# A hybrid decoder layer on one core: scores of two attention units in a row, a new order of the attention stage's groups, and another set of first transfers

## The chip, the cores and the metric

One core of a Trainium2 chip runs the whole layer as one program. The metric is the device time of one execution in microseconds (us), lowest is best; the time before is the median of three runs. The profile is of one further execution. The engines are named as in the profile: PE (TensorE matmul), PEld (its weight loads), DVE (VectorE), ACT (ScalarE), POOL (GpSimd) and SP (SyncE, which here only issues transfers).

## The reference

One layer on x of 512 positions by 1024 channels, float32, cut to what matters:

```python
x = x + 0.5 * swiglu(rms_norm(x, ffn1_norm), ...)            # d_ff 2816
h = rms_norm(x, mix_norm)
xr, gate, q, k, v = split(h @ w_in)                          # 512 columns each
y_rnn = rg_lru(conv(xr), gates) * gelu(gate)
qh, kh = rms_norm(heads(q)) / 8, rms_norm(heads(k))          # 8 heads of 64
z = qh @ kh.T ; causal = k_pos < q_pos                       # stick-breaking attention
tail = reverse_cumsum(where(causal, log_sigmoid(-z), 0)) - itself
w = where(causal, exp(log_sigmoid(z) + tail), 0) ; y_att = w @ v
x = x + concat(rms_norm(y_rnn), rms_norm(y_att)) @ w_out
x = x + 0.5 * swiglu(rms_norm(x, ffn2_norm), ...)
```

## The kernel before

Everything is held transposed: channels on the 128 partitions, the 512 positions along the free axis, x as eight tiles `x[k]` of 128x512. Every float32 product is three matmuls on a high and a low part of each operand (`mm3`: high-high, low-high, high-low). ACT makes the high parts, DVE the low parts.

**The start.** `first_products()` computes gate and up products of the first three 128-column blocks of the first FFN, six PSUM banks at once, while weights and x arrive. It issues, for `kk` = 0 to 3, `x[2*kk]`, six pieces of weights of 128x256 (`raw[i]`, alternately from the gate and the up matrix) and `x[2*kk+1]`, all over SP's queue. A tile `vec` (128x66) holds the norm gains, convolution weights and biases; it comes over ACT's queue. The first products need the high part of `x[0]`, which ACT computes with a gain out of `vec` (`xh_a`, L157), and the high parts of the weights (`first_h`: DVE makes that of piece 0, ACT that of piece 1). Ahead of them PE runs `WARM` matmuls of 128x128 float32 on constants (each is two matmul records in the profile). SP then goes on with the weights of the FFN.

**The attention stage.** The eight heads are taken in four pairs. A unit is the query blocks 3, or 2, or 1 and 0 of one pair of heads, so there are twelve units, in the order 3_0, 2_0, 1_0, 3_2, 2_2, 1_2, 3_4 and so on to 1_6 (the first query block, then the first head of the pair; the program's tile names end in the same way). `STEPS` is a string written by hand; its letters set the order on PE, and `step()` keeps each group behind the one before:

- Z, `weigh`: scores of one unit, for two heads at once, each on 64 of the 128 rows of the PE array; a bfloat16 matmul (`fut_b`) adds the mask. Two banks of the four of tag "z". ACT then writes `s` (sigmoid of -z) and `be` (sigmoid of z), DVE a scan (`rest`, L971) and a product into `be` (L979). There are three buffers for `be`, two for `s`.
- W, `turn_weights`: the unit's weights are transposed on PE (128x128 matmuls, 6 or 8 of them, into two banks of tag "w") and copied by ACT into `wt` (L999).
- P, `attend`: values times weights of one pair, after the pair's three W; 16 matmuls into the one bank of tag "y". ACT makes `yah` (L1019) and a square of it, DVE `yal` (L1022).
- F: the recurrent half of the output projection for one block of 128 columns, 12 matmuls into the one bank of tag "o" (the second F takes a "w" bank), copied out by ACT (`yr`, L1061) and added to `x[k]` by DVE (L1062).
- C, `begin`: the attention half for a block of columns, but for the last pair of heads, 9 matmuls, into a "z" bank. S and R are the sums for the last norm and their spreading.

The order of instructions on ACT and DVE is not written out: the framework's scheduler lays it down when the program is built, and each engine then works strictly through its own list.

Of the kernel before, what the change touches and what calls it, by code (L numbers as in the profile page):

```python
# [8 lines left out]
F32 = mybir.dt.float32  # L9
# [6 lines left out]
P = 128  # L16
T = 512
D = 1024
KD = D // P
# [16 lines left out]
LATE = 3  # L36

WIDE = {p: "gu" if p in (6, 9) else "g" for p in range(PLAIN // 2, NF // 2)}
WARM = 9

STEPS = "ZFZFZWZFWZWFZWZPWZFWZWZPWZFWZWPWFCWFPCCSCR"


C_G1, C_GM, C_G2 = 0, 8, 16
# [2 lines left out]
NVEC = 66  # L50
# [3 lines left out]
def hybrid_layer_kernel(  # L54
    ctx: ExitStack,
    tc: tile.TileContext,
    xT: bass.AP,
    vecs: bass.AP,
    wg1: bass.AP,
    wu1: bass.AP,  # L60
    wd1: bass.AP,
# [9 lines left out]
    nc = tc.nc  # L71

    const = ctx.enter_context(tc.tile_pool(name="const", bufs=1))
    wpool = ctx.enter_context(tc.tile_pool(name="wpool", bufs=3))
    xpool = ctx.enter_context(tc.tile_pool(name="xpool", bufs=1))
# [14 lines left out]
    def f32(ap):  # L90
        return ap.bitcast(F32)

    def bank(name, tag="b"):
        return banks["pool"].tile([P, T], F32, tag=tag, name=name, bufs=banks["tags"][tag])
# [1 line left out]

    mhalf = const.tile([P, 8], F32, tag="mhalf", name="mhalf")
    nc.vector.memset(mhalf, -0.5)
    vec = const.tile([P, NVEC], F32, tag="vec", name="vec")
    nc.scalar.dma_start(vec, vecs)  # L100
    warm = const.tile([P, 8], F32, tag="warm", name="warm")
    nc.scalar.activation(warm, mhalf, AF.Sigmoid)
    ones = const.tile([P, P], F32, tag="ones", name="ones")
# [16 lines left out]
        halves_b.append(t)  # L120
    ident_b, fut_b = halves_b

    x = [xpool.tile([P, T], F32, tag=f"x{k}", name=f"x{k}") for k in range(KD)]


    def weights(src, name, n=KD * P, rows=1):
# [400 lines left out]
    pt = bank("warm")  # L527
    for _ in range(WARM):
        nc.tensor.matmul(pt[:, :P], ones, ones, start=True, stop=True)
    n1 = Normed("a")  # L530

    def first_products():

        with tc.tile_pool(name="first", bufs=1, reuse_waits="tile") as fi:
            ws = [(w, f) for f in range(3) for w in (wg1, wu1)]
            raw, hi, lo, pts = [], [], [], []
            last = None
            for i in range(len(ws)):
                raw.append(fi.tile([P, KD * P], F32, tag=f"wr{i}", name=f"first_r{i}"))
                hi.append(fi.tile([P, KD * P], F32R, tag=f"wh{i}", name=f"first_h{i}"))  # L540
                lo.append(fi.tile([P, KD * P], F32R, tag=f"wl{i}", name=f"first_l{i}"))
                pts.append(bank(f"first_p{i}", "by"[i // 4]))
            for kk in range(KD // 2):
                s = slice(2 * kk * P, (2 * kk + 2) * P)
                nc.sync.dma_start(x[2 * kk], xT[:, 2 * kk, :])
                for i, (w, f) in enumerate(ws):
                    nc.sync.dma_start(raw[i][:, s], w[f // 2][:, f % 2 * KD * P :][:, s])
                nc.sync.dma_start(x[2 * kk + 1], xT[:, 2 * kk + 1, :])
            for kk in range(KD // 2):
                s = slice(2 * kk * P, (2 * kk + 2) * P)  # L550
                ks = (2 * kk, 2 * kk + 1)
                for k in ks:
                    n1.add(x[k], vec[:, C_G1 + k : C_G1 + k + 1], k)
                    if k == ks[0]:
                        for i in range(len(ws)):
                            if i == 0 or kk == 0 and i % 2 == 0:
                                nc.vector.tensor_copy(hi[i][:, s], raw[i][:, s])
                            else:
                                copied = nc.scalar.copy(hi[i][:, s], raw[i][:, s])
                                last = copied if kk == 1 else last  # L560
                        for i in range(len(ws)):
                            nc.vector.tensor_sub(lo[i][:, s], raw[i][:, s], f32(hi[i][:, s]))
                if kk == KD // 2 - 2:
                    with tc.issue_after(last.ins):
                        for k in range(KD):
                            n1.square(x[k], k, nc.vector)
                for k in ks:
                    s = slice(k * P, (k + 1) * P)
                    if k == KD - 1:
                        n1.rsqrt(D)  # L570
                    for wp, xp in ((hi, n1.h), (hi, n1.l), (lo, n1.h)):
                        if k == KD - 1 and wp is lo:
                            n1.spread()
                        for i in range(len(ws)):
                            nc.tensor.matmul(  # L575
                                pts[i],
                                wp[i][:, s],
                                xp[k],
                                start=k == 0 and wp is hi and xp is n1.h,
                                stop=k == KD - 1 and wp is lo,  # L580
                            )
        return [(pts[i], pts[i + 1]) for i in range(0, len(ws), 2)]
# [3 lines left out]
    def into(norm, c, squares=True):  # L586
# [5 lines left out]
        return done  # L592

    ffn("a", n1, wg1, wu1, wd1, first_products, into(nm, C_GM))


# [305 lines left out]
    with tc.tile_pool(name="att", bufs=2, reuse_waits="tile") as ap:  # L902
# [5 lines left out]
        for qbs in ((3,), (2,), (1, 0)):  # L908
            w = sum(qb + 1 for qb in qbs) * P
            m = ap.tile([P, 2 * w], F32, tag=f"m{qbs[0]}", name=f"marks{qbs[0]}", bufs=1)  # L910
            nc.gpsimd.memset(m, 0.0)
            for head in range(2):
                c = head * w
# [117 lines left out]
        def next_weights(c):  # L1031
            if not pending[c]:
                pending[c].extend(weights_out((len(out_r), len(begun))[c], c, 2))
            return pending[c].pop(0)
# [8 lines left out]

        for what in STEPS:
            if what == "Z":
# [7 lines left out]
            elif what == "F":  # L1053
                w = next_weights(0)
# [4 lines left out]
                k = len(out_r)  # L1059
# [20 lines left out]
        for k in range(KD):  # L1080
            if k == len(begun):
                begin("zw"[k % 2])
            pt, w = begun[k]
# [15 lines left out]


_INS = [
    "xT", "vecs", "wg1", "wu1", "wd1", "w_rg", "w_qkv", "w_gate", "w_out", "wg2", "wu2", "wd2",
]


def _layout(x, ffn1_norm, ffn1_w_gate, ffn1_w_up, ffn1_w_down, mix_norm, w_in,
            conv_w, conv_b, rg_w_a, rg_b_a, rg_w_x, rg_b_x, rg_lambda,
            q_norm, k_norm, rnn_out_norm, attn_out_norm, w_out,
            ffn2_norm, ffn2_w_gate, ffn2_w_up, ffn2_w_down):
    import numpy as np  # L1110

    def cols(v):
        return np.asarray(v).reshape(-1, P).T

    def by_block(w):

        k, n = w.shape
        return w.reshape(k // P, P, n // P, P).transpose(2, 1, 0, 3).reshape(n // P, P, k)

    def by_pairs(w):  # L1120


        o = by_block(w).reshape(NF, P, KD, P)
        o = np.concatenate([o[:, :, 0::2], o[:, :, 1::2]], axis=2).reshape(NF, P, KD * P)
        o = np.concatenate([o[1::2], o[0::2]], axis=2)
        b = by_block(w)
        o[: PLAIN // 2] = np.concatenate([b[0:PLAIN:2], b[1:PLAIN:2]], axis=2)
        return o

    w = np.asarray(w_in)[0]  # L1130
    qkv = w[:, 2 * DR :].reshape(KD // 2, 2, P, 3, DR).transpose(3, 0, 2, 1, 4)
    def gates(a, x):

        a, x = np.asarray(a)[0], np.asarray(x)[0]
        o = np.empty((P, NJ, P), a.dtype)
        for n in range(2 * NJ):
            r = (n % 2) * HD
            o[r : r + HD, n // 2, r : r + HD] = a[n]
            o[r : r + HD, n // 2, HD - r : 2 * HD - r] = x[n]
        return o.reshape(P, NJ * P)  # L1140

    def swapped(v):

        return np.asarray(v).reshape(-1, 2, HD)[:, ::-1].reshape(-1)

    vecs = np.concatenate(
        [
            cols(ffn1_norm[0]), cols(mix_norm[0]), cols(ffn2_norm[0]), cols(conv_w[0]),
            cols(conv_b[0]), cols(rg_b_a[0]), cols(swapped(rg_b_x[0])), cols(rg_lambda[0]),
            cols(rnn_out_norm[0]), cols(attn_out_norm[0]),  # L1150
            cols(np.tile(np.asarray(q_norm[0]), 2)), cols(np.tile(np.asarray(k_norm[0]), 2)),
        ],
        axis=1,
    )

    a = {
        "xT": np.asarray(x)[0].T.reshape(KD, P, T).transpose(1, 0, 2),
        "vecs": vecs,
        "w_rg": by_block(w[:, : 2 * DR]),
        "w_qkv": qkv.reshape(3, KD // 2, P, 2 * DR),  # L1160
        "w_gate": gates(rg_w_a, rg_w_x),
        "w_out": by_block(np.asarray(w_out)[0]),
        "wg1": by_pairs(np.asarray(ffn1_w_gate)[0]),
        "wu1": by_pairs(np.asarray(ffn1_w_up)[0]),
        "wd1": by_block(np.asarray(ffn1_w_down)[0]),
        "wg2": by_pairs(np.asarray(ffn2_w_gate)[0]),
        "wu2": by_pairs(np.asarray(ffn2_w_up)[0]),
        "wd2": by_block(np.asarray(ffn2_w_down)[0]),
    }
    return {n: np.ascontiguousarray(a[n]) for n in _INS}  # L1170
# [21 lines left out]
```

## Time and profile before

| what | value |
|---|---|
| runs | 899.58, 899.85, 899.93 us; median 899.85 |
| profiled execution | 900.1 us, of which 898.3 us are the span from the first to the last instruction |
| PE busy | 893.8 us (99%) |
| DVE, ACT, POOL busy | 712.9 (79%), 467.0 (52%), 72.9 us (8%) |
| 471.50 to 526.00 us (attention stage): PE, DVE, ACT busy | 54.50, 48.12, 43.20 us of 54.50 |
| 0 to 5 us: DMA share of its 16 engines | 0.55 |

Reading it: times are microseconds from the span's start. In a timeline row the first number is the start, the second the duration, `x2` counts merged records, and a bracket gives the engine's idle time before and who ended it. Matmuls overlap on PE, so what one costs is the distance to the next start and not its duration.

### The profile page before, as it was taken

The page shows a single profiled execution, that of the slowest core. Times are in us where ns is not written, and L with a number is a line of the kernel's source. Part 1 is how long each engine was busy: PE and PEld are TensorE (multiplying, and loading weights), DVE is VectorE, ACT ScalarE, POOL GpSimd, SP SyncE. Part 2 cuts the span into 40 slices and gives each one's busy share as a digit, 9 for nine tenths or more (in the row PEclk, how much of TensorE's full clock was granted, in tenths as well). Part 3 has the DMA queues.
Part 4 walks back from the last instruction along what each step waited for, and adds up shares of the span by engine and source line. Part 5 has one row for each costly group of instructions (what it writes and reads, how often), then busy time and mean ns, then how long its engine had stood idle before and what let it go on. Part 6 is the DMA issues. An engine that isn't in the chain of part 4 may idle for free.

```text
span 898.3 us, 12600 instructions
## 1 busy us (share of the span) xinstructions
PE 893.8 (99%) x4882; PEld 763.2 (85%) x4882; DVE 712.9 (79%) x1032; ACT 467.0 (52%) x771; POOL 72.9 (8%) x60
## 2 busy tenths in 40 slices
PE   9999999999999999999999999999999999999998
PEld 8888899888998888887877678888899988998887
DVE  8599789877887668758689949698689877897763
ACT  7255365544553446365768834454256544563450
POOL 0000000000000005444140001400000000000000
PEclk9999999999999999999999999999999999999999
DMA  8314322341232221322231012324322332233302
GB/s 279 115 55 149 114 94 94 130 147 53 94 130 82 88 94 66 134 71 96 69 113 53 24 47 94 118 70 147 117 94 94 130 128 72 94 113 100 89 24 93
DMA packets 27595, 89.18 MB, mean 99 GB/s; under 512 B 2960, under 2 KB 6288, under 8 KB 23440
## 3 DMA queue, kind: packets, MB, share of 16 engines
q1 hardware_dynamic: 27392, 88.35, 29.3%
q8 instruction: 38, 0.62, 0.3%
q14 instruction: 21, 0.17, 0.1%
q10 hardware_dynamic: 144, 0.03, 0.0%
HBM read 86.28 MB, written 2.10 MB: 98 GB/s over the span
## 4 chain that ended last, share of the span: by engine, by line
PE 95%; DVE 2%; ACT 1%; issue 0%; POOL 0%
PE pxub L397 5%; PE pxua L397 5%; PE pxgb L397 5%; PE pxga L397 5%; PE pdb L144 4%; PE pdb L143 4%; PE pdb L145 4%; PE pda L143 4%; PE pda L144 4%; PE pda L145 4%; PE pyua L397 4%; PE pyub L397 4%; PE first_p L575 4%; PE pygb L397 4%; PE pyga L397 4%; PE po L143 2%
## 5 line engine op out<-in xcount | busy, mean ns | idle before, releaser
L144 PE MATMUL pdb<-hlb,h_db 128*128 128x512 f32 (+2 forms) x180 | 69.2, 386 | 0.0
L145 PE MATMUL pdb<-hhb,l_db 128*128 128x512 f32 (+2 forms) x180 | 68.9, 386 | 0.0
L143 PE MATMUL pdb<-hhb,h_db 128*128 128x512 f32 (+2 forms) x180 | 68.5, 386 | 0.0
L144 PE MATMUL pda<-hla,h_da 128*128 128x512 f32 x176 | 68.4, 390 | 0.0
L145 PE MATMUL pda<-hha,l_da 128*128 128x512 f32 x176 | 68.0, 390 | 0.0
L143 PE MATMUL pda<-hha,h_da 128*128 128x512 f32 x176 | 67.2, 390 | 0.0
L482 DVE SCALAR_TENSOR_TENSOR x<-pdb,x 128x512 f32<-128x512 f32 (+2 forms) x33 | 21.8, 672 | 33.3 <-PE pdb L145 33.3
L133 ACT CAST h_da<-r_da 128x768 fp32r<-128x768 f32 (+1 forms) x28 | 24.2, 869 | 39.7 <-PE pda L144 14.7
L133 ACT CAST h_db<-r_db 128x768 fp32r<-128x768 f32 (+1 forms) x28 | 24.2, 868 | 38.6 <-PE pdb L144 21.1
L482 DVE SCALAR_TENSOR_TENSOR x<-pda,x 128x512 f32<-128x512 f32 x32 | 21.6, 687 | 22.6 <-PE pda L145 22.6
L145 PEld LDWEIGHTS pdb<-hhb,l_db 128*128 128x128 f32 x180 | 33.8, 188 | 6.7
L144 PEld LDWEIGHTS pdb<-hlb,h_db 128*128 128x128 f32 x180 | 33.8, 188 | 6.3
L143 PEld LDWEIGHTS pdb<-hhb,h_db 128*128 128x128 f32 x180 | 33.9, 188 | 6.0
L145 PEld LDWEIGHTS pda<-hha,l_da 128*128 128x128 f32 x176 | 33.0, 188 | 6.9
L144 PEld LDWEIGHTS pda<-hla,h_da 128*128 128x128 f32 x176 | 33.1, 188 | 6.3
L143 PEld LDWEIGHTS pda<-hha,h_da 128*128 128x128 f32 x176 | 33.1, 188 | 6.2
L173 POOL TENSOR_TENSOR sqa_m<-sqa_m,sq_m 128x512 f32<-128x512 f32 x7 | 11.8, 1680 | 310.2 <-ACT sq_m L172 310.0
L377 ACT CAST h_gb<-rgb 128x512 fp32r<-128x512 f32 (+1 forms) x24 | 18.3, 764 | 24.0 <-PE pdb L144 12.4
L135 DVE TENSOR_TENSOR l_da<-r_da,h_da 128x768 fp32r<-128x768 f32 (+1 forms) x28 | 27.7, 991 | 3.0 <-ACT h_da L133 3.0
L377 ACT CAST h_ua<-rua 128x512 fp32r<-128x512 f32 (+1 forms) x24 | 18.3, 763 | 22.6 <-PE pyga L397 8.8
L135 DVE TENSOR_TENSOR l_db<-r_db,h_db 128x768 fp32r<-128x768 f32 (+1 forms) x28 | 27.7, 991 | 3.0 <-ACT h_db L133 3.0
L377 ACT CAST h_ub<-rub 128x512 fp32r<-128x512 f32 (+1 forms) x24 | 18.3, 764 | 22.2 <-PE pygb L397 8.8
(453 smaller groups left out, 2825.2 us busy)
## 6 DMA issues: line engine op xcount, KB each, us to landing
r_da<-in_wd SPq DMA_DIRECT2D x24, 384.0 KB, 3.1
r_db<-in_wd SPq DMA_DIRECT2D x24, 384.0 KB, 3.1
rga<-in_wg SPq DMA_DIRECT2D x8, 1024.0 KB, 5.6
rua<-in_wu SPq DMA_DIRECT2D x8, 1024.0 KB, 4.7
rgb<-in_wg SPq DMA_DIRECT2D x8, 1024.0 KB, 5.3
rub<-in_wu SPq DMA_DIRECT2D x8, 1024.0 KB, 4.8
r_o<-in_w_out SPq DMA_DIRECT2D x8, 512.0 KB, 3.2
r_gb<-in_wg SPq DMA_DIRECT2D x6, 512.0 KB, 3.4
```

Source lines behind the costliest of these rows:

```text
L133: nc.scalar.copy(hi, raw)
L135: nc.vector.tensor_sub(lo, raw, f32(hi))
L143: nc.tensor.matmul(out_, wh, ah, start=start, stop=False)
L144: nc.tensor.matmul(out_, wh, al, start=False, stop=False)
L145: return nc.tensor.matmul(out_, wl, ah, start=False, stop=stop)
L173: (engine or nc.gpsimd).tensor_add(self.acc, self.acc, sq)
L377: nc.scalar.copy(hi[:, to], a)
L397: nc.tensor.matmul(pt[:, : r.shape[1]], l[:, s], r, start=start and (k, i) == order[0], stop=(k, i) == order[-1], skip_group_check=True,)
L482: nc.vector.scalar_tensor_tensor(x[k][:, t], pt[:, t], 0.5, x[k][:, t], op0=ALU.mult, op1=ALU.add)
L575: nc.tensor.matmul(pts[i], wp[i][:, s], xp[k], start=k == 0 and wp is hi and xp is n1.h, stop=k == KD - 1 and wp is lo,)
```

## The change

Four edits. The vectors no longer have a transfer of their own: they are packed behind the first block of x in memory, and the tile `x0` becomes 128x578, with `vec` its last 66 columns. The first piece of weights goes over ACT's queue, where the vectors' transfer was. `WARM` is 8 instead of 9. And `STEPS` is another string with the same letters: scores of two units stand in a row at six places, and turns and projections alternate between them.

```diff
-WARM = 9
+WARM = 8
-STEPS = "ZFZFZWZFWZWFZWZPWZFWZWZPWZFWZWPWFCWFPCCSCR"
+STEPS = "ZZFFZZWFWFWZZPWFWZZWFWZZPWFWZZPWFWCWPCCSCR"
...
-    vec = const.tile([P, NVEC], F32, tag="vec", name="vec")
-    nc.scalar.dma_start(vec, vecs)
...
+    x0 = xpool.tile([P, T + NVEC], F32, tag="x0", name="x0")
+    vec = x0[:, T:]
+    x = [x0[:, :T]] + [xpool.tile([P, T], F32, tag=f"x{k}", name=f"x{k}") for k in range(1, KD)]
...
-                nc.sync.dma_start(x[2 * kk], xT[:, 2 * kk, :])
+                c = 2 * kk * T + NVEC
+                if kk == 0:
+                    nc.sync.dma_start(x0, xT[:, : T + NVEC])
+                else:
+                    nc.sync.dma_start(x[2 * kk], xT[:, c : c + T])
                 for i, (w, f) in enumerate(ws):
-                    nc.sync.dma_start(raw[i][:, s], w[f // 2][:, f % 2 * KD * P :][:, s])
-                nc.sync.dma_start(x[2 * kk + 1], xT[:, 2 * kk + 1, :])
+                    queue = nc.scalar if kk == i == 0 else nc.sync
+                    queue.dma_start(raw[i][:, s], w[f // 2][:, f % 2 * KD * P :][:, s])
+                nc.sync.dma_start(x[2 * kk + 1], xT[:, c + T : c + 2 * T])
```

Lines after the start move by up to five: L1007 of before is L1012 of after, L988 is L993. The number at the end of a name is the buffer's.

On PE, just ahead of the last unit's turn (`pw1_0`, `pw1_1`), before:

```order
L145 MATMUL po1_0_4986<-yah2_4941,l_o1_0_4984 128x512
L988 MATMUL pw1_0_4996<-ident_75,be1_6_4910 128x128 x3
L988 MATMUL pw1_1_4997<-ident_75,be1_6_4910 128x128 x3
L143 MATMUL po0_7_5008<-yrh0_4293,h_o0_6_4960 128x512
L144 MATMUL po0_7_5008<-yrl0_4295,h_o0_6_4960 128x512
L145 MATMUL po0_7_5008<-yrh0_4293,l_o0_6_4962 128x512
```

The same place on PE, now:

```order
L145 MATMUL po1_0_4999<-yah2_4946,l_o1_0_4997 128x512
L993 MATMUL pw1_0_5009<-ident_73,be1_6_4929 128x128 x3
L993 MATMUL pw1_1_5010<-ident_73,be1_6_4929 128x128 x3
L1012 MATMUL py3_5021<-wt6_4953,v0_4349 64x512
L1012 MATMUL py3_5021<-wt7_4954,v0_4349 64x512
L1012 MATMUL py3_5021<-wt6_4953,v1_4351 64x384
```

Before, the twelve matmuls of the last F (`po0_7`) stood between the turn and the last `attend` (`py3`); now that `attend` follows the turn directly.

On PE, the turn of unit 3_4 (`be3_4`), now:

```order
L143 MATMUL po0_5_4743<-yrh3_4305,h_o0_4_4659 128x512
L144 MATMUL po0_5_4743<-yrl3_4307,h_o0_4_4659 128x512
L145 MATMUL po0_5_4743<-yrh3_4305,l_o0_4_4661 128x512
L993 MATMUL pw3_0_4761<-ident_73,be3_4_4702 128x128 x4
L993 MATMUL pw3_1_4762<-ident_73,be3_4_4702 128x128 x4
L942 MATMUL pz1_4_4773<-kTh_3360,qTh_3358 128x256
```

Before, six groups lay between the scores of 3_4 and its turn (P W Z F W Z); now three do (Z W F), and the turn stands ahead of the scores of 1_4 (`pz1_4`) instead of behind them.

On DVE, around `yal1` (from the second `attend`), before:

```order
L971 SCALAR_TENSOR_TENSOR rest1_4_4770<-s1_4_4768,marks1_4374 128x767
L979 TENSOR_TENSOR be1_4_4769<-be1_4_4769,rest1_4_4770 128x767
L971 SCALAR_TENSOR_TENSOR rest3_6_4805<-s3_6_4803,marks3_4368 128x1023
L979 TENSOR_TENSOR be3_6_4804<-be3_6_4804,rest3_6_4805 128x1023
L173 TENSOR_TENSOR sqa_t_4678<-sqa_t_4678,sq_t1_4824 128x512
L1022 SCALAR_TENSOR_TENSOR yal1_4823<-py1_4812,vec_69,yah1_4821 128x512
L971 SCALAR_TENSOR_TENSOR rest2_6_4852<-s2_6_4850,marks2_4371 128x767
```

and now:

```order
L135 TENSOR_TENSOR l_o1_4_5133<-r_o1_4_5129,h_o1_4_5131 128x1024
L1067 TENSOR_TENSOR x5_98<-yr5_4756,x5_98 128x512
L976 SCALAR_TENSOR_TENSOR rest1_4_4797<-s1_4_4795,marks1_4371 128x767
L984 TENSOR_TENSOR be1_4_4796<-be1_4_4796,rest1_4_4797 128x767
L976 SCALAR_TENSOR_TENSOR rest3_6_4818<-s3_6_4816,marks3_4365 128x1023
L984 TENSOR_TENSOR be3_6_4817<-be3_6_4817,rest3_6_4818 128x1023
L173 TENSOR_TENSOR sqa_t_4640<-sqa_t_4640,sq_t1_4837 128x512
L1027 SCALAR_TENSOR_TENSOR yal1_4836<-py1_4825,x0_93,yah1_4834 128x512
L1067 TENSOR_TENSOR x6_99<-yr6_4870,x6_99 128x512
```

`yal1` still stands behind the two units 1_4 and 3_6, but a weight split (`l_o1_4`) and an addition (`x5`) that stood behind it before now stand ahead of them.

More of the change, by code (lines that the diff above doesn't have):

```diff
@@ L57, in hybrid_layer_kernel @@
     xT: bass.AP,
-    vecs: bass.AP,
     wg1: bass.AP,
@@ L121, in hybrid_layer_kernel @@
     ident_b, fut_b = halves_b
-    x = [xpool.tile([P, T], F32, tag=f"x{k}", name=f"x{k}") for k in range(KD)]
+    x0 = xpool.tile([P, T + NVEC], F32, tag="x0", name="x0")
+    vec = x0[:, T:]
+    x = [x0[:, :T]] + [xpool.tile([P, T], F32, tag=f"x{k}", name=f"x{k}") for k in range(1, KD)]
     def weights(src, name, n=KD * P, rows=1):
@@ L1101 @@
 _INS = [
-    "xT", "vecs", "wg1", "wu1", "wd1", "w_rg", "w_qkv", "w_gate", "w_out", "wg2", "wu2", "wd2",
+    "xT", "wg1", "wu1", "wd1", "w_rg", "w_qkv", "w_gate", "w_out", "wg2", "wu2", "wd2",
 ]
@@ L1154, in _layout @@
     )
+    xt = np.asarray(x)[0].T.reshape(KD, P, T).transpose(1, 0, 2).reshape(P, KD * T)
     a = {
-        "xT": np.asarray(x)[0].T.reshape(KD, P, T).transpose(1, 0, 2),
-        "vecs": vecs,
+        "xT": np.concatenate([xt[:, :T], vecs, xt[:, T:]], axis=1),
         "w_rg": by_block(w[:, : 2 * DR]),
```

## The prediction

> **What bounds the kernel now.** I read the waits first, then the windows of the attention stage, then PE's timeline there row by row, and last the timeline of VectorE (DVE), ScalarE (ACT) and of the first 8 us.
>
> ```profile
> PE warm L529 <- DVE ones L104: 1.1, 1, 1.1
> PE ptk L821 <- DVE natk L803: 0.6, 1, 0.6
> 471.50:526.00 54.50, 54.50 (x396) 39.95 (x397) 48.12 (x42) 43.20 (x100) 0.00 (x0) 1.00 0.12 43
> ```
>
> PE waits twice in the whole program, for 1.1 and 0.6 us. In the attention stage (third row: length, then busy time of PE, PEld, DVE and ACT) PE is busy for all of 54.50 us, DVE for 48.12 and ACT for 43.20. So the time is the sum of PE's own distances from one matmul to the next, and it can fall only if those shrink. DVE has 6 us to spare in 54: a new order on PE that wants DVE's results sooner runs into it.
>
> How long a group of matmuls takes on PE is the distance to the start of the next group:
>
> ```profile
> 475.24 0.39 PE L145 MATMUL po<-yrh,l_o 128*128 128x512 f32 x1
> 475.56 0.44 PE L937 MATMUL pz<-kTh,qTh 64*128 64x384 f32 x2
> ...
> 476.18 0.28 PE L951 MATMUL pz<-fut_b,ident_b 64*128 64x128 bf16 x4
> 476.40 0.50 PE L143 MATMUL po<-yrh,h_o 128*128 128x512 f32 x1
> ...
> 479.35 0.38 PE L937 MATMUL pz<-kTh,qTh 64*128 64x256 f32 x2
> ...
> 479.81 0.29 PE L951 MATMUL pz<-fut_b,ident_b 64*128 64x128 bf16 x4
> 479.90 0.36 PE L937 MATMUL pz<-kTh,qTh 64*128 64x256 f32 x2
> ...
> 480.56 1.09 PE L988 MATMUL pw<-ident,be 128*128 128x128 f32 x8
> 481.58 0.49 PE L937 MATMUL pz<-kTh,qTh 64*128 64x512 f32 x2
> ...
> 482.60 0.50 PE L143 MATMUL po<-yrh,h_o 128*128 128x512 f32 x1
> ...
> 485.46 0.82 PE L988 MATMUL pw<-ident,be 128*128 128x128 f32 x6
> 486.21 0.44 PE L937 MATMUL pz<-kTh,qTh 64*128 64x384 f32 x2
> ...
> 514.58 2.37 PE L1007 MATMUL py<-wt,v 128*64 128x512 f32 x16
> 516.89 0.87 PE L988 MATMUL pw<-ident,be 128*128 128x128 f32 x6
> 517.52 0.47 PE L143 MATMUL po<-yrh,h_o 128*128 128x512 f32 x1
> ...
> 520.37 0.39 PE L143 MATMUL po<-yah,h_o 128*128 128x512 f32 x1
> ...
> 522.41 0.82 PE L988 MATMUL pw<-ident,be 128*128 128x128 f32 x6
> 522.98 0.47 PE L143 MATMUL po<-yrh,h_o 128*128 128x512 f32 x1
> ```
>
> The reader is to see that the same group costs more or less by its neighbours. Nine matmuls of 512 columns take 522.41 − 520.37 = 2.04, so one takes 0.227 and the twelve of an F 2.72. Six turns between two groups on 128 rows take 522.98 − 522.41 = 0.57, so one takes 0.095. Everything above that is the price of a boundary:
>
> - F to Z: 475.56 − 475.24 = 0.32 against 0.227: 0.09. Z to F: an F between two Z takes 479.35 − 476.40 = 2.95, less 2.72 and 0.09: 0.14.
> - W to Z: 486.21 − 485.46 = 0.75 against 0.57: 0.18. Z to W: eight turns between two Z take 481.58 − 480.56 = 1.02, less 8 × 0.095 and 0.18: some 0.06.
> - W to F: 520.37 − 517.52 = 2.85 against 2.72: 0.13. F to W next to nothing.
> - Z to Z: the last mask is followed after 479.90 − 479.81 = 0.09 by the next scores, and after 476.40 − 476.18 = 0.22 by anything else: −0.13, and −0.01 at the entry.
>
> **What the two orders make of it.** Counted in the two strings, before there are 5 F-Z, 3 Z-F, 5 Z-W, 8 W-Z and 3 W-F: 0.45 + 0.42 + 0.30 + 1.44 + 0.39 = 3.0 us, with 0.3 for single ones at the `attend` groups. Now there are 6 Z-Z (−0.84), 1 F-Z, 1 Z-F, 2 Z-W, 4 W-Z and 6 W-F: 0.09 + 0.14 + 0.12 + 0.72 + 0.78 − 0.84 = 1.0, again with 0.3 for single ones. The groups themselves are the same, so PE's own work in the stage gets **2.0 us** shorter.
>
> **What the new order makes PE wait for.** Before, the scan and the product of each unit were hidden by several groups on PE. The rows that tell the chain of a unit, DVE first:
>
> ```profile
> 507.04 0.96 DVE L979 TENSOR_TENSOR be<-be,rest 128x767 f32<-128x767 f32 x1
> 508.10 2.29 DVE L971 TENSOR_TENSOR_SCAN rest<-s,marks 128x1023 f32<-128x1023 f32 x1
> 510.52 1.23 DVE L979 TENSOR_TENSOR be<-be,rest 128x1023 f32<-128x1023 f32 x1
> 511.66 0.69 DVE L173 TENSOR_TENSOR sqa_t<-sqa_t,sq_t 128x512 f32<-128x512 f32 x1
> 512.26 0.75 DVE L1022 SCALAR_TENSOR_TENSOR yal<-py,vec,yah 128x512 fp32r<-128x512 f32 x1
> 512.92 1.75 DVE L971 TENSOR_TENSOR_SCAN rest<-s,marks 128x767 f32<-128x767 f32 x1
> ...
> 515.68 1.22 DVE L135 TENSOR_TENSOR l_o<-r_o,h_o 128x1024 fp32r<-128x1024 f32 x1
> 473.21 1.08 ACT L965 ACTIVATE s<-pz 128x512 f32<-128x512 f32 x2
> 476.50 0.87 ACT L965 ACTIVATE s<-pz 128x384 f32<-128x384 f32 x2 [0.25 <-PE pz L951]
> 485.67 0.59 ACT L1061 COPY yr<-po 128x512 f32<-128x512 f32 x1 [0.42 <-PE po L145]
> 522.93 0.99 ACT L999 COPY wt<-pw 128x256 f32<-128x256 f32 x4 [1.78 <-PE pw L988]
> ```
>
> On DVE a unit of 1023 columns takes 511.66 − 508.10 = 3.56 until the next instruction, one of 767 takes 515.68 − 512.92 = 2.76, a scan right behind a product 508.10 − 507.04 = 1.06 where the 0.96 alone would give about 0.87, so 0.19 more. ACT starts 476.50 − 476.40 = 0.10 after the scores end.
>
> 1. *The turn of 3_4* has now only the scores of 2_4, a turn and an F behind the scores of 3_4. Cover: 0.71 (476.40 − 475.56 = 0.84, less 0.13 as it follows scores) + 0.63 (517.52 − 516.89) + 2.86 = 4.20. Chain: 0.10 + 1.08 (both `s`) + 3.65 (scan start to product end, 510.52 + 1.23 − 508.10) = 4.83. Wait: **0.6**. Before, six groups lay there.
> 2. *The third `attend`* writes the one bank of tag "y", which is free when `yal1` has read the second's result. DVE then has, from the scan of 3_4 on: 3.56 + 0.19 + 2.76 for 3_4 and 2_4, 1.13 for `l_o1_4` (1.22 less the 0.09 by which neighbours overlap), 0.60 for `x5` (as the square, 512.26 − 511.66), 2.76 + 0.19 + 3.56 for 1_4 and 3_6, 0.60 for the square and 0.75 for `yal1`: 16.1, and 1.18 from the end of the scores to the scan: 17.3. PE in the meantime: 4.20, wait 0.63, turn 0.97, scores of 1_4 (480.56 − 479.35 = 1.21, less 0.13) and 3_6 (482.60 − 481.58 = 1.02), `attend` 2.31 (516.89 − 514.58), turn 0.63, F 2.86, turn 0.75, scores 0.71 and 1.21: 16.4. Wait: **0.9**. Here the saturated engine is DVE: each us that PE saves is asked back from it.
> 3. *The last `attend`* stood behind an F and now stands directly behind the last unit's turn. Its values come through ACT's copies, which end 522.93 + 0.99 − 522.41 = 1.51 after the turn's start; the turn takes 0.57, with 0.18 for the entry of the `attend`. Wait: **0.8**.
> 4. *The third F* writes the "o" bank that the F before it has just left: its copy ends 485.67 + 0.59 − 485.46 = 0.80 after that F's end, and one turn of 0.57 lies between. Wait: **0.2**.
>
> Together 2.5 us. The bounds: no one of the four can be below 0, and with half of the two that lean on DVE (its products' ends are read from single rows) the sum is 1.7; if the 0.12 that DVE idles between a scan and its product were to come twice it is 3.2.
>
> **The start.**
>
> ```profile
> 1.08 4.21 PE L529 MATMUL warm<-ones 128*128 128x128 f32 x18 [1.08 <-DVE ones L104]
> 4.95 1.23 PE L575 MATMUL first_p<-xh_a,first_h 128*128 128x512 f32 x2
> 5.98 1.04 PE L575 MATMUL first_p<-xl_a,first_h 128*128 128x512 f32 x2
> 6.83 0.66 PE L575 MATMUL first_p<-xh_a,first_l 128*128 128x512 f32 x2
> 7.33 0.63 PE L575 MATMUL first_p<-xh_a,first_h 128*128 128x512 f32 x2
> 3.90 0.72 ACT L157 ACTIVATE xh_a<-x,vec 128x512 fp32r<-128x512 f32 x1 [1.23 <-DMA vec<-in_vecs]
> 4.93 0.41 ACT L559 CAST first_h<-first_r 128x256 fp32r<-128x256 f32 x1 [0.31 <-DMA first_r<-in_wu]
> 1.18 0.42 SPq L547 DMA_DIRECT2D first_r<-in_wg  x1
> ```
>
> The first product waits for `xh_a`, which waits for `vec`; the second for ACT's cast of the second piece (the up matrix), which ends at 5.34. Until about 6.83 two matmuls take 0.85 (5.98 to 6.83), then 0.50 (6.83 to 7.33): the clock rises there. With the first piece of weights on ACT's queue, the second piece moves up one place on SP's queue, where an issue takes 0.42 (the last row, of the first piece), and what the packed `x0` gains by one transfer fewer it gives back by longer rows. I take 0.3 us earlier for the second product, at a moment when a matmul costs twice what it costs later: 0.3 × (0.227 / 0.43) = **0.15** gained; ends +0.2 (packed `x0` lands 0.4 later, and the first product with it) and −0.4 (the full 0.42 and as much for the first product). The warm matmul taken out ends PE's warming 0.4 earlier and delays nothing, since the product waits for data.
>
> Sum: −2.0 + 2.5 − 0.15 = +0.35. The profiled execution took 900.1 (span 898.3 and 1.8 around it), 0.25 above the median of 899.85; the forecast on the median is **900.2**. About 0.2%, 1.8 us, is what a measurement of this kernel can tell from no change.
>
> **The rivals.**
>
> *A, boundaries only.* The four waits don't come, because copies, scans and `yal1` are done sooner than single rows make me think. For it: PE waits nowhere in this stage now, and ACT idles 11 of 54.5 us. Against it: all four are chains of one instruction behind the other, and the last (0.8) has nothing between its ends but ACT's copies. Time: 899.85 − 2.0 − 0.15 = 897.7. It decides from the point where fewer than 0.35 of the 2.5 us remain.
>
> The Trainium skill, page "TensorEngine Tiling (Array Packing)", section "Key Properties", says that a change of the tiling mode drains TensorE; groups Z (64-row matmuls) and the others are such modes. The trace agrees with 0.06 to 0.18 us a boundary. By that rule alone, with the boundaries cut from 23 to 11, the time would be rival A's 897.7; it says nothing of the engines that then fall behind, which is why it speaks for the gain and not for the total.
>
> *B, the clock rises later (slower).* It rose 5.75 us after the first warm matmul (6.83 − 1.08). In the new start the warm matmuls end 0.4 earlier, so PE idles up to 0.4 before the first product. If such a gap made the count begin anew, the rise would come 5.75 after a first product at about 4.85, at 10.6, and 3.77 us more at half rate would cost 3.77 × (1 − 0.227/0.43) = 1.8: 902.0. Against it: before, too, PE paused near 4.9 and 5.4 without harm. It decides if the gap is what the clock counts.
>
> The Trainium skill, page "TensorE: Matmul & The Clock Gate", section "Part 1: The HAM clock gate (the "warmup" mystery)", has the clock released by one busy window of about 3.4 us of a free-running count. The rise at 6.83 with PE busy from 1.08 fits a window begun at 3.4; whether 0.4 us of idling spoils one, no run here shows. If it does, the next window would end at 10.2, and the time would be rival B's within 0.2.
>
> *C, banks of the scores (slower).* Two units in a row need all four "z" banks, and the second needs those that ACT must still read. If ACT has a copy of weights (0.99) and one of F (0.59) ahead of that reading, PE waits some 1.6 more, once: 901.8. Against it: ACT's 43.2 of 54.5.
>
> That the start does nothing is no rival for the sum: 0 for −0.15.
>
> **How the numbers follow.** Forecast with its waits 0.72, A 0.12, B 0.08, C 0.08. The forecast's own range: waits 1.7 to 3.2 and start −0.4 to +0.2 give −0.7 to +1.4, 899.1 to 901.25; with the boundaries 2.0 ± 0.3 it is 898.8 to 901.5. With C it reaches 901.9, which leaves out A and B, 0.2. Faster than 898.05 is A, 0.12; slower than 901.65 are B and C, 0.16; the rest, 0.72, is within.
>
> **What would show it.** Right: in the profile of the changed kernel the waits list PE behind `be` of 3_4, behind `yal1` at the third `attend`, behind `wt` at the last and behind `yr` at the third F; an F between two turns takes about 2.85; the last `attend` starts 0.5 us later than now. Rival A: PE has no wait there, and the last `attend` starts 2 us earlier. B: two of the first matmuls still take 0.85 after 7 us. C: a wait of a Z for `be` or `s` on ACT. The forecast is wrong if DVE's list is worked through faster than its rows before, or if a boundary between two groups on 128 rows costs more than the 0.13 that I give it.

## The result: slower, 908.8 against 899.8 us

The changed kernel takes 908.83 us (median of 5 runs, 908.63 to 909.07), the kernel before 899.84 (5 runs); the ratio is 1.0101 with a 95% interval of 1.0086 to 1.0115. The forecast was 900.2, with 898.8 to 901.9 as its range.

The profile after, first the page's line of busy times, then all of PE's waits:

```profile
PE 901.0 (99%) x4880; PEld 758.1 (84%) x4880; DVE 712.9 (79%) x1032; ACT 466.9 (51%) x771; POOL 72.9 (8%) x60
```

```profile
PE warm L529 <- DVE ones L101: 1.1, 1, 1.1
PE py L1012 <- DVE yal L1027: 0.8, 1, 0.8
PE pw L993 <- DVE be L984: 0.6, 1, 0.6
PE first_p L580 <- ACT xh_a L157: 0.5, 1, 0.5
PE py L1012 <- ACT wt L1004: 0.3, 1, 0.3
```

PE's waits have grown by 1.6 us, but its busy time by 7.2 (901.0 against 893.8), with the same groups of matmuls and the same clock. The reader is to see that most of the loss is no wait. Where it arises is told by the start of each stage on PE (from the timelines, differences taken before rounding; the last two columns belong to experiments below). The plain products of an FFN have 512 columns (L143 to L145); of its L397 products most have 256:

| PE reaches | before | after | difference | one distance for all (e9) | string alone (e3) |
|---|---|---|---|---|---|
| first products | 4.95 | 5.22 | +0.27 | +0.42 | 0.00 |
| plain products of the first FFN | 39.96 | 39.80 | -0.16 | -0.12 | 0.00 |
| its L397 products | 105.35 | 107.07 | +1.72 | -0.12 | 0.00 |
| the last of these | 330.38 | 332.14 | +1.76 | -0.12 | 0.00 |
| q | 374.34 | 377.22 | +2.88 | -0.12 | 0.00 |
| attention's first scores | 471.58 | 475.79 | +4.20 | -0.13 | -0.03 |
| sums for the last norm | 532.42 | 537.72 | +5.31 | +0.56 | +0.71 |
| L397 products of the second FFN | 648.84 | 657.29 | +8.45 | +0.56 | +0.71 |
| end | 895.48 | 904.41 | +8.93 | +0.56 | +0.71 |

Most of it comes in stages that the diff doesn't touch, as 1.4 to 2.9% of their length, and none in the 225 us of the L397 products. The windows from 50 to 100 us, before and then after (the second number is PE's busy time, with its matmuls in brackets):

```profile
50.00:100.00 50.00, 50.00 (x222) 41.39 (x222) 47.44 (x84) 22.98 (x42) 0.00 (x0) 1.00 0.44 141
```

```profile
50.00:100.00 50.00, 50.00 (x216) 40.17 (x215) 45.85 (x82) 22.62 (x42) 0.00 (x0) 1.00 0.42 136
```

In the same 50 us, with PE busy throughout and the granted clock at 1.00, stand 216 matmuls for 222: one of 512 columns takes 0.2333 us where it took 0.2267. The 256-column ones in the L397 stage, before and then after, got faster (a pair, a single one and the next pair):

```profile
138.29 0.40 PE L397 MATMUL pxua<-xl_sa,h_ua 128*128 128x256 f32 x2
138.53 0.28 PE L397 MATMUL pxua<-xl_sa,l_ua 128*128 128x256 f32 x1
138.65 0.40 PE L397 MATMUL pxua<-xl_sa,h_ua 128*128 128x256 f32 x2
```

```profile
135.44 0.40 PE L397 MATMUL pxua<-xh_sa,h_ua 128*128 128x256 f32 x2
135.68 0.28 PE L397 MATMUL pxua<-xh_sa,l_ua 128*128 128x256 f32 x1
135.79 0.40 PE L397 MATMUL pxua<-xh_sa,h_ua 128*128 128x256 f32 x2
```

Three take 0.36 before and 0.35 after; over 998 of the up products that follow each other within a bank the means are 0.1196 and 0.1168. That is why this stage, with slower 512-column matmuls beside them, comes out even.

What the change does to every product is to move tiles. Without `vec` the constants are 288 bytes shorter in each partition (space is given out in pieces of 32 bytes), so all weights' tiles lie 288 bytes lower. `x0` is 288 bytes longer, so x's later tiles and all that follows lie where they were. The first products, whose weights lie in a space behind x's, keep their 0.227 in the changed kernel, and an `attend`, whose tiles all lie there, takes 2.31 in both; every product of 512 columns that takes its weights (or, as q, k and v do, its moving columns) from the tiles that moved lost the 0.227. The experiments below give each product's distance as the address of its weights minus that of its moving tile, modulo 256 bytes: 0 before for all these, -32 after (+32 for q, k, v).

### The profile page after: what moved, and what is told of

Read it like the earlier page. It is cut to its first block, busy times and chain, and to the rows that moved or that the text cites. A ratio compares the mean times of both kernels' runs of the same rounds, so it can differ in the third digit from the quotient of the medians.

```text
span 907.1 us, 12596 instructions
## 1 busy us (share of the span) xinstructions
PE 901.0 (99%) x4880; PEld 758.1 (84%) x4880; DVE 712.9 (79%) x1032; ACT 466.9 (51%) x771; POOL 72.9 (8%) x60
## 4 chain that ended last, share of the span: by engine, by line
PE 98%; DVE 1%; DMA 0%; issue 0%; ACT 0%; DVEq 0%
PE pxua L397 5%; PE pxub L397 5%; PE pxgb L397 5%; PE pxga L397 5%; PE pdb L144 5%; PE pdb L145 5%; PE pdb L143 5%; PE pda L144 5%; PE pda L145 5%; PE pda L143 5%; PE pyua L397 4%; PE pyga L397 4%; PE pygb L397 4%; PE pyub L397 4%; PE first_p L580 4%; PE po L143 2%
## 5 line engine op out<-in xcount | busy, mean ns | idle before, releaser
L145 PE MATMUL pdb<-hhb,l_db 128*128 128x512 f32 (+2 forms) x180 | 69.7, 391 | 0.0
L143 PE MATMUL pdb<-hhb,h_db 128*128 128x512 f32 (+2 forms) x180 | 69.3, 391 | 0.0
L145 PE MATMUL pda<-hha,l_da 128*128 128x512 f32 x176 | 68.9, 395 | 0.0
L143 PE MATMUL pda<-hha,h_da 128*128 128x512 f32 x176 | 68.0, 395 | 0.0
L145 PEld LDWEIGHTS pdb<-hhb,l_db 128*128 128x128 f32 x180 | 33.8, 188 | 7.7
L143 PEld LDWEIGHTS pdb<-hhb,h_db 128*128 128x128 f32 x180 | 33.8, 188 | 6.9
L145 PEld LDWEIGHTS pda<-hha,l_da 128*128 128x128 f32 x176 | 33.0, 187 | 7.9
L143 PEld LDWEIGHTS pda<-hha,h_da 128*128 128x128 f32 x176 | 33.0, 188 | 7.1
```

Source lines behind the costliest of these rows:

```text
L143: nc.tensor.matmul(out_, wh, ah, start=start, stop=False)
L145: return nc.tensor.matmul(out_, wl, ah, start=False, stop=stop)
```

## Experiments

Labels e1 to e12 follow the order of the runs. The kernel before, run beside them, took 899.68 to 900.00.

**e1: weights and moving tiles at the same remainder of 64.**

```diff
+    pad = const.tile([P, 8], F32, tag="pad", name="pad")
+    nc.vector.memset(pad, 0.0)
     warm = const.tile([P, 8], F32, tag="warm", name="warm")
-    x0 = xpool.tile([P, T + NVEC], F32, tag="x0", name="x0")
-    vec = x0[:, T:]
+    x0 = xpool.tile([P, T + 80], F32, tag="x0", name="x0")
+    vec = x0[:, T : T + NVEC]
```

> The changed kernel with 32 bytes added ahead of `warm` and the tile `x0` made 592 columns wide instead of 578, so that weights and moving tiles again lie at the same remainder of 64 bytes, as before the change. Theory A (address: when a product's weights and its moving tile lie 32 bytes apart modulo 64, 512 columns take 0.2333 us instead of 0.2267 and 256 columns 0.117 instead of 0.120): 899.0 to 900.2, pace 0.227 everywhere. Theory B (the new start or the new order puts PE into a slower pace whatever the addresses): 908.8, pace 0.233 from 40 us on.

898.67 us (ratio 0.9988, 0.9979 to 0.9997): the loss is gone, against theory B. But the time lies under theory A's 899.0 to 900.2, and the pace is not 0.227 everywhere, as it said: 512 columns take 0.2291 in the down projections and 0.2333 in q, k, v, and 256 columns 0.1162. The distance is -64 here, so 64 bytes are not the period.

**e2, e4: the kernel before, only shifted.** In e2 the same pad stands in x's tiles, in e4 ahead of `warm`.

```diff
+    pad = xpool.tile([P, 8], F32, tag="pad", name="pad")
+    nc.vector.memset(pad, 0.0)
     x = [xpool.tile([P, T], F32, tag=f"x{k}", name=f"x{k}") for k in range(KD)]
```

> The kernel before with nothing but 32 bytes added between the weights' tiles and x's tiles, so that every moving tile and the first weights move by 32 bytes and the other weights don't. Theory A: 908 to 910, pace 0.233 from 40 us on and 0.227 in the first products. Theory B: 899.9. Theory C (what counts is where the weights lie alone, remainder 0 being slow): 900.5 to 901, only the first products slower, since their weights alone move to remainder 0.

> The kernel before with 32 bytes added ahead of `warm`, so that weights and moving tiles all move by 32 bytes together, to remainder 0 of 64. Theory A (the difference counts): 899.9, pace 0.227. Theory C (weights at remainder 0 are slow): 908 to 910.

e2 takes 908.41 (1.0097, 1.0081 to 1.0112) and e4 899.71 (0.9999, 0.9990 to 1.0008). The windows of both, e2 first:

```profile
50.00:100.00 50.00, 50.00 (x216) 40.17 (x215) 45.95 (x82) 22.18 (x42) 0.00 (x0) 1.00 0.42 141
```

```profile
50.00:100.00 50.00, 50.00 (x223) 41.40 (x222) 47.25 (x83) 22.98 (x42) 0.00 (x0) 1.00 0.41 142
```

32 bytes of padding that nothing reads bring the whole loss, with order and start as before; the same 32 bytes under both tiles bring nothing. So the difference of the two addresses decides (theory A), not a place of its own (C), not order or start (B). e2's distance is 0 - 32, the changed kernel's 0 - 288, and their paces agree to 0.0001: a period of 256 bytes.

**e3: the string alone**, with start and addresses as before.

```diff
-STEPS = "ZFZFZWZFWZWFZWZPWZFWZWZPWZFWZWPWFCWFPCCSCR"
+STEPS = "ZZFFZZWFWFWZZPWFWZZWFWZZPWFWZZPWFWCWPCCSCR"
```

> The kernel before with the new string of groups alone; start and addresses as before. The prediction's sum: boundaries -2.0, waits +2.5, so 900.3. The profile of the changed kernel shows waits of only 1.7 there, and the stage's growth of 0.56 with about 0.75 of slower matmuls in it: by that 899.6. Theory B in the form that the new order is what makes PE slow: 907 or more.

900.65 us (1.0010, 1.0002 to 1.0019) beside 899.74: +0.9, in the profile +0.71 by the end of the stage. The prediction's sum gave +0.5; my correction in the expectation, to 899.6, was the worse reading: it put the growth of the stage in the changed kernel at 0.56, where the table above has 5.31 - 4.20 = 1.11.

**e5 to e8: other distances.** The kernel before, with 96, 128, 160 and 192 bytes between the weights' tiles and x's:

```diff
+    pad = xpool.tile([P, 24], F32, tag="pad", name="pad")   # e5; 32, 40 and 48 in e6, e7, e8
+    nc.vector.memset(pad[:, :8], 0.0)
```

> The kernel before with 96 bytes between the weights' tiles and x's, so that weights minus moving tile is -96 bytes modulo 256 (for the q, k, v products, where the two change places, +96). If the pace repeats every 64 bytes: as 32 bytes, 908. If it goes by 128 bytes: -96 is +32, again near 908 (0.233). If it goes by 256 bytes or more, it is a place not seen yet: pace between 0.227 and 0.235.

> The same with 128 bytes, weights minus moving tile 128 modulo 256 for all. Period 64 or 128: 899.7 as before, pace 0.227 and 0.120. Longer period: another pace; the slow ones at 32 and 64 bytes would make some 0.229 to 0.233 likely, 902 to 908.

> The same with 160 bytes, weights minus moving tile +96 modulo 256 (q, k, v -96). Period 64: 908. Period 128: as 32 bytes, 908. With 256: the counterpart of the run with 96 bytes, with q, k, v and the rest changing roles.

> The same with 192 bytes, weights minus moving tile +64 modulo 256 (q, k, v -64). Period 64: 899.7. With 256: the aligned kernel's q, k, v, at +64, took 0.2333 there, and its other products, at -64, 0.2290; so here the roles change: 907 to 909, with q, k, v at 0.229.

913.78, 909.59, 912.85 and 903.39 us. No run is at 899.7, so periods of 64 and 128 fall. The expectation for e8 (907 to 909) missed: its 256-column products, faster than in any run so far, give 2.4 us back in the first FFN alone. Sorted by distance, with means over 989 distances between matmuls (down projections), 271 (q, k, v) and 998 (L397, 256 columns):

| weights minus moving tile | 512 columns, down | 512 columns, q, k, v | 256 columns |
|---|---|---|---|
| 0 (before, e4) | 0.2278 | 0.2272 | 0.1196 |
| +32 | | 0.2333 (after) | |
| +64 | 0.2330 (e8) | 0.2333 (e1) | 0.1138 (e8) |
| +96 | 0.2342 (e7) | 0.2342 (e5) | 0.1184 (e7) |
| 128 | 0.2327 (e6) | 0.2327 (e6) | 0.1186 (e6) |
| -96 | 0.2333 (e5) | 0.2334 (e7) | 0.1198 (e5) |
| -64 | 0.2291 (e1) | 0.2304 (e8) | 0.1162 (e1) |
| -32 | 0.2333 (after) | | 0.1168 (after) |

In q, k, v the roles are exchanged (weights from x's tiles, the moving tile from the weights' tiles), and at the five signed distances that both have, beside 0, the paces agree to 0.0013. That is strong evidence that it is the distance that counts, and not which tile lies where. The pair of +32 and -32 has only one of the two each.

**e9: the whole change at distance 0.** As e1, but with `x0` 640 columns wide.

```diff
-    x0 = xpool.tile([P, T + NVEC], F32, tag="x0", name="x0")
+    x0 = xpool.tile([P, T + P], F32, tag="x0", name="x0")
```

> The changed kernel, whole, with 32 bytes ahead of `warm` and `x0` made 640 columns wide, so that weights minus moving tile is 0 modulo 256 bytes for every product, as in the kernel before. Theory A (all that the prediction missed is the pace that goes by this difference): the order's +0.7 of the run with the string alone and the start's -0.2, so 900.3, the middle of the program as long as before to 0.1. Rival (the start or the packed tile costs or gains something of its own in the middle): anything else, with matmuls of the middle off 0.2267.

900.49 us (1.0006, 0.9997 to 1.0015), and the middle of the program is as long as before to 0.01 us (table above). Its window from 50 to 100 us:

```profile
50.00:100.00 50.00, 50.00 (x222) 41.43 (x221) 47.23 (x84) 23.07 (x42) 0.00 (x0) 1.00 0.44 141
```

222 matmuls again. So 908.83 - 900.49 = 8.3 us of the 9.0 are the distance, and 0.6 all four edits.

**e10 to e12: each product at its best distance.** By the table, 512 columns want 0 and 256 columns +64. e10 keeps the high and low tiles in one block of 16 slots, so that those of the L397 products can begin 192 bytes (48 floats) later:

```diff
+    def slot(c, shift=0):
+        o = (taken[c] % 8 + 8 * (c == "l")) * T + shift
+        taken[c] += 1
+        return ring[:, o : o + T]
...
-                        xpool.tile([P, 2, TH], F32R, tag=f"x{c}", name=f"x{c}_{n}", bufs=8) for c in "hl"
+                        slot(c, 48).rearrange("p (c t) -> p c t", c=2) for c in "hl"
```

(and the six `xb` tiles likewise, out of one block). e11 has another shift for each family of products, in steps finer than 32 bytes.

> The kernel before, order and start unchanged, in which only the moving tiles of the L397 products are shifted by 192 bytes, so that weights minus moving tile is +64 there and 0 everywhere else. Theory A: the 256-column products there (some 1520) go from 0.1192 to 0.1141, -7.8, the 512-column ones (some 600) from 0.2312 to 0.2323, +0.7; so 892.6, between 890 and 894. Rival (the pace hangs on the absolute place of both tiles or on what else uses the memory then): no gain, 899 to 900.

> The same kernel with steps finer than 32 bytes, another one for each family of products: weights minus moving tile -16 for the first products and those of the first FFN ahead of L397, -8 for the recurrent and gate columns, +8 for q, k, v, +16 for the output projection, -48 for the second FFN's ahead of L397, +64 and +48 for L397's of the first and second FFN. If the pace goes by whole 32 or 64 byte pieces, -16, -8, 8 and 16 act as 0 or as 32 (0.2267 or 0.2333); if it is finer, some value lies under 0.2267.

In both, slots are written anew in the order of the code: the second FFN's high and low parts of x[4] to x[7] overwrite operands that the output projection still reads, and PE waits for them; what the two kernels compute is no longer the layer. e10's waits have it:

```profile
PE po L151 <- ACT ring L165: 10.3, 3, 6.6
```

Their totals, 908.36 and 926.30 us, therefore tell nothing, and only the pace of matmuls is read from them. In e10 the first FFN's end comes 3.45 us earlier than before, its 256-column products at 0.1145 (0.1138 in e8). In e11, 512 columns take 0.2321 at -16, 0.2327 at -8, 0.2332 at -48, 0.2307 at +8 and 0.2355 at +16 (there 0.2287 at 0), and the 256-column products at +48 take 0.1191: none of these was better than 0 and +64. e12 is e10 with those parts written later:

```diff
-            done(k)
+            for kk in (range(4, KD) if k == KD - 1 else [k] if k < 4 else []):
+                done(kk)
```

> As the run with the moving tiles of the L397 products shifted by 192 bytes (weights minus moving tile +64 there, 0 everywhere else), but the high and low parts of x[4] to x[7] for the second FFN are written only when the output projection has read its last operands, so that nothing is overwritten early; each engine has its instructions in the order of the kernel before. By what the other showed up to 470 us (first FFN 3.45 us shorter, everything else as before), two FFNs give -6.9: 892.9, between 892 and 894. Rival (the waits of 10 us at the output projection stay): 903.

**892.86 us** (5 runs, 892.66 to 893.37; ratio 0.9922, 0.9909 to 0.9936): faster than both kernels. The L397 products of e12:

```profile
137.10 0.39 PE L407 MATMUL pxua<-ring,h_ua 128*128 128x256 f32 x2
137.32 0.28 PE L407 MATMUL pxua<-ring,l_ua 128*128 128x256 f32 x1
137.44 0.39 PE L407 MATMUL pxua<-ring,h_ua 128*128 128x256 f32 x2
```

Three take 0.34 where they took 0.36 (mean 0.1146 against 0.1196), and the plain stage keeps its count, with busy time down and no new wait:

```profile
50.00:100.00 50.00, 50.00 (x222) 41.40 (x222) 47.80 (x84) 23.19 (x42) 0.00 (x0) 1.00 0.42 142
```

```profile
PE 886.8 (100%) x4882; PEld 755.2 (85%) x4882; DVE 711.6 (80%) x1032; ACT 466.7 (52%) x771; POOL 72.9 (8%) x60
```

## Why the prediction was wrong, step by step

**The step that failed** is the sum itself: -2.0 + 2.5 - 0.15 has a term for the attention stage and one for the start, and none for the 800 us between and behind them. "The groups themselves are the same" was taken for "their pace is the same". The packing edit was costed as a transfer alone, though it also moves every weights' tile; the missing term is +8.3 us (908.83 - 900.49). No rival held it either: all three were about waits or the clock. What the rest of the sum was worth is seen in e9, 900.49 for a forecast of 900.2. The prediction's own warning, that with PE busy all the time only its distances count, pointed at it: 0.227 was read from rows and then taken as a constant.

**Boundaries, -2.0, and waits, +2.5: right, and well sized.** Rows of the changed kernel, PE and then ACT:

```profile
489.12 0.82 PE L993 MATMUL pw<-ident,be 128*128 128x128 f32 x6
489.96 0.50 PE L143 MATMUL po<-yrh,h_o 128*128 128x512 f32 x1
...
493.61 0.44 PE L942 MATMUL pz<-kTh,qTh 64*128 64x384 f32 x2
...
495.53 2.37 PE L1012 MATMUL py<-wt,v 128*64 128x512 f32 x16
...
504.67 0.48 PE L143 MATMUL po<-yrh,h_o 128*128 128x512 f32 x1
...
508.34 1.06 PE L993 MATMUL pw<-ident,be 128*128 128x128 f32 x8 [0.63 <-DVE be L984]
...
517.99 0.44 PE L942 MATMUL pz<-kTh,qTh 64*128 64x384 f32 x2
...
520.77 2.38 PE L1012 MATMUL py<-wt,v 128*64 128x512 f32 x16 [0.79 <-DVE yal L1027]
...
523.92 0.48 PE L143 MATMUL po<-yrh,h_o 128*128 128x512 f32 x1
...
526.80 0.82 PE L993 MATMUL pw<-ident,be 128*128 128x128 f32 x6
...
529.56 0.82 PE L993 MATMUL pw<-ident,be 128*128 128x128 f32 x6
530.67 2.81 PE L1012 MATMUL py<-wt,v 128*64 128x512 f32 x16 [0.30 <-ACT wt L1004]
533.42 0.51 PE L143 MATMUL po<-yah,h_o 128*128 128x512 f32 x1
```

```profile
489.32 0.59 ACT L1066 COPY yr<-po 128x512 f32<-128x512 f32 x1
530.08 0.99 ACT L1004 COPY wt<-pw 128x256 f32<-128x256 f32 x4 [1.02 <-PE pw L993]
```

What a wait costs is again read from distances between starts; the idle time in a bracket is less, since matmuls overlap.

1. The turn of 3_4 starts 508.34 - 504.67 = 3.67 after the F ahead of it, where an F between two turns takes 526.80 - 523.92 = 2.88: 0.8 (predicted 0.6).
2. The third `attend` starts 520.77 - 517.99 = 2.78 after the scores ahead of it, the first one 495.53 - 493.61 = 1.92 after the same kind of scores: 0.9 (0.9).
3. The last `attend` starts 1.11 after the turn instead of 0.75, and then takes 533.42 - 530.67 = 2.75 instead of 2.31, since the copies still arrive while it runs, until 530.08 + 0.99 = 531.07: 0.36 + 0.44 = 0.8 (0.8, thought of as one wait ahead of it).
4. The third F starts 489.96 - 489.12 = 0.84 after its turn instead of 0.57 to 0.63: 0.2 to 0.3 (0.2). PE's waits don't list it; the copy out of its bank ends just ahead of it, at 489.32 + 0.59 = 489.91.

Together 2.7 to 2.8; in e3, with the addresses of before, each of the four is the same to 0.05. With the string alone the stage grew by 0.71 in the profile, so the boundaries gave 2.0 to 2.1 for the predicted 2.0. Two slips of the working: the string of before has 5 Z-F and 3 F-Z, and not the other way round, which makes the boundaries 2.1; and 2.5 with twice 0.12 is 2.7, so the 3.2 of the upper bound doesn't follow. Rival A is refuted: all four waits came.

**The start, -0.15: not shown, its working wrong.** The prediction let the first product wait for `xh_a`. In its own rows that was done at 3.90 + 0.72 = 4.62, and the product at 4.95 follows the warm matmuls without idle time: they set its start. In the changed kernel it does wait. `xh_a` starts 0.55 us later (4.45, waiting for the packed `x0`, against 3.90, waiting for `vec`), beyond my bound of 0.4:

```profile
1.08 3.67 PE L529 MATMUL warm<-ones 128*128 128x128 f32 x16 [1.08 <-DVE ones L101]
5.22 0.80 PE L580 MATMUL first_p<-xh_a,first_h 128*128 128x512 f32 x2 [0.47 <-ACT xh_a L157]
6.15 0.73 PE L580 MATMUL first_p<-xl_a,first_h 128*128 128x512 f32 x2
```

```profile
4.45 0.72 ACT L157 ACTIVATE xh_a<-x 128x512 fp32r<-128x512 f32 x1 [1.78 <-DMA x<-in_xT]
5.07 0.39 ACT L564 CAST first_h<-first_r 128x256 fp32r<-128x256 f32 x1
```

The first product comes 0.27 later, not earlier, and the cast for the second, thought to come 0.3 earlier, now stands right behind `xh_a` and ends at 5.07 + 0.39 = 5.46, against 5.34. Nor is a matmul saved at half rate a gain by itself. In e3, with the start of before, two products take 0.47 from 5.76 on, a pace that before has only from 7.33 on, and its plain stage still begins at 39.96, as before; PE then waits for a cast of weights:

```profile
5.76 0.63 PE L575 MATMUL first_p<-xl_a,first_h 128*128 128x512 f32 x2
6.23 0.62 PE L575 MATMUL first_p<-xh_a,first_l 128*128 128x512 f32 x2
...
7.46 0.50 PE L575 MATMUL first_p<-xh_a,first_h 128*128 128x512 f32 x1 [0.37 <-ACT first_h L559]
```

The plain stage of the changed kernel begins 0.16 sooner, e9's 0.12. With the start of before it begins anywhere from 39.33 (e4) to 40.25 (e2; e11 left out, whose first products are slower), so the sign of this term stays open.

**Rival B is refuted**, by e1 rather than by the changed kernel. In the latter PE idled 0.47 us ahead of the first product, but that product's row is at full rate already (0.80 for two, against 1.23 before), so the clock had risen ahead of the idle time or in it. In e1, with the same start, the clock was still low behind a gap of 0.34: the first product takes 0.79, where e2's, at full rate, takes 0.49 (last rows below). By rival B full rate would come 5.75 after it, at 11.0; from 6.91 on two products take 7.37 - 6.91 = 0.46:

```profile
5.24 0.79 PE L582 MATMUL first_p<-xh_a,first_h 128*128 128x512 f32 x1 [0.34 <-ACT xh_a L159]
...
6.91 0.62 PE L582 MATMUL first_p<-xh_a,first_h 128*128 128x512 f32 x2
7.37 0.63 PE L582 MATMUL first_p<-xl_a,first_h 128*128 128x512 f32 x2
```

The Trainium skill, page "TensorE: Matmul & The Clock Gate", section "Part 1: The HAM clock gate (the "warmup" mystery)", has it that the window runs free of the kernel's start; the fourteen profiles agree: with PE busy from 1.08 to 1.11 on in all of them, the last matmul at half rate began between 3.6 and 6.5 us. In e2, whose start is that of the kernel before, the 18 warm matmuls take 3.61 where before they took 4.21, and the first product starts at 4.71 instead of 4.95:

```profile
1.08 3.61 PE L531 MATMUL warm<-ones 128*128 128x128 f32 x18 [1.08 <-DVE ones L104]
4.71 0.49 PE L577 MATMUL first_p<-xh_a,first_h 128*128 128x512 f32 x1
```

**Rival C**: no wait of a Z for ACT appears in PE's waits. Refuted.

**What stays open** is the mechanism behind the distance. The loads of weights do run under the matmul before them; one row of each from the changed kernel:

```profile
50.37 0.40 PE L143 MATMUL pua<-xh_a,h_ua 128*128 128x512 f32 x1
```

```profile
50.37 0.19 PEld L144 LDWEIGHTS pua<-xl_a,h_ua 128*128 128x128 f32 x1
```

So PE reads weights and moving columns at the same time, and a clash of the two reads that depends on their addresses would fit all runs. The Trainium skill, page "SBUF — State Buffer", section "Who interferes with whom", counts two read ports for PE, one for each, and calls them independent; the measurement differs, 0.2278 to 0.2342 us for the same matmuls (down projections) by the distance of the two tiles alone. No run took the loads away, nor the other engines' work on the same tiles, so the clash itself is argued and not shown.

## What to carry to other kernels

Where PE is busy all the time, a change that adds, removes or widens any tile can alter the pace of the matmuls, as 32 bytes did in e2: list the addresses of weights and moving tiles before and after, and cost the difference with the number of matmuls, as one costs a wait. Before judging an edit by its time, run it once with padding that restores the distances; here that turned +9.0 into +0.6. And the distance is a thing to be tuned by itself, by size of product: it gave 7 us without moving one instruction.

## What the hardware showed unexpectedly

The time of a 128x128 by 128x512 fp32r product depends on the address of its weights minus that of its moving tile modulo 256 bytes: in the down projections 0.2278 us at 0, up to 0.2342 at +96. For 256 columns the best of the distances measured is another one: 0.1138 at +64 (0.1146 in e12), 0.1196 at 0. And the clock rises at a time that differs by up to 3 us between executions of programs whose first matmuls start alike: the last one at half rate began at 3.6 in e2 and at 6.5 in e11.
